# One shared priority, and a shorter planned lag, for the small operations of an inverse square root

## The chip, the cores and the metric

The kernel runs on one core of a Trainium2 chip. The metric is the device time of one execution in microseconds (us); the figure for the kernel before is the median of three runs. One more execution was profiled, and all rows below come from it.

## The reference

Two models of two layers each run on 256 tokens of width 1024, one behind the other. What matters here is that both normalise often, each time with 1/sqrt of a sum of squares:

```python
def rms_norm(x, g):
    xf = x.astype(jnp.float32)
    y = xf * lax.rsqrt(jnp.mean(xf * xf, -1, keepdims=True) + NORM_EPS)
    return (y * g.astype(jnp.float32)).astype(x.dtype)
...
    kk = kk / jnp.maximum(jnp.sqrt(jnp.sum(kk * kk, -1, keepdims=True)), 1e-12)    # rwkv7, per head
    y = (y - mean) * lax.rsqrt(var + RWKV_GN_EPS) * hv(ln_g) + hv(ln_b)            # rwkv7, per head
    o = ((o - mean) * lax.rsqrt(var + RET_GN_EPS)).reshape(b, s, h * dv) * gn_g.astype(f32)   # retention
...
    for l in range(DEPTH):                                   # first model
        h = rms_norm(x, attn_norm_g[l])
        ... attention over chosen keys, rwkv7, pooling, retention, gates, merge ...
        h2 = rms_norm(x, mlp_norm_g[l])
        x = x + jnp.square(jax.nn.relu(h2 @ mlp_up[l])) @ mlp_down[l]
```

The second model has the same kind of norms (of rows, of heads, of latents) around a gated delta rule with block attention, a latent attention, and two layers that mix many small experts ("peer").

## The kernel before

The activations stay on the chip; weights stream in as tiles of 128x1024 (tile `raw`). ScalarE rounds each tile into a high part (`hi`), VectorE takes the rest (`lo = raw - hi`), and TensorE multiplies three times (`hT`,`hi`; `lT`,`hi`; `hT`,`lo`) into PSUM tiles `mm` and `sm`. The instruction rows of TensorE are 128x256 matmuls nearly throughout.

In the span of the profiled execution the stages lie so: 20 to 440 us the mix of layer 0 of the first model, 470 to 660 its MLP, 660 to 1080 the mix of layer 1, 1080 to 1310 its MLP, 1310 to 1515 the gated delta rule and block attention of the second model, 1515 to 2360 the first peer layer, 2360 to 2495 the latent attention, 2495 to 3343 the second peer layer.

**An inverse square root is a chain of small VectorE operations.** `rsqrt` (line 467) is 10 operations that each need the one before: a bit trick, then three Newton steps; the last one writes the result spread out to 128x256 (`wide`). `head_rsqrt` puts one more ahead (`v`, which reads the sums from PSUM). `rstd` (line 586) does it for whole rows in 15 operations, of which two independent ones always stand together. There are 35 such chains: 20 of `head_rsqrt` (tile `h`, ten in each mix of the first model), 3 of `unit` in the delta rule (tiles `g8v`, `g8r`, `g8t`), 10 of `rstd` (tile `rs`), 2 of `unit` in the latent attention. Below they are numbered 0 to 34 in the order of VectorE's program.

**What sets the order.** The program is written as generators (rwkv7, attention, retention, the gates and so on), and a `Plan` gives every operation a planned start and end while it is issued: a cost by its size, and `LAG` (0.3 us) from the end of an operation of VectorE or ScalarE until its result counts as ready. Two orders come out of that:

- On VectorE and ScalarE a scheduler orders the instructions by the priority that `Noted.call` sets, the planned start (`cur_priority = 1000 + int(start * 1000)`); one that is not ready by the scheduler's reckoning lets a later one pass. So operations of other generators come to stand between two operations of a chain. They are called fillers below.
- TensorE's order is the order of issue. `weave` (line 775) takes up a generator when the planned time of TensorE reaches the time that the generator has yielded. `head_rsqrt` yields the end of its chain by the plan plus `HM` and then issues the transposes of the wide result, which need the whole chain:

```python
        s.rsqrt(rs, v, tm, wide)
        wide = wide.rearrange("p (t n e) f -> p t n (e f)", t=2, n=n)
        yield s.plan.last + s.HM
        ps = s.sm((P, n, S))
        for j in range(n):
            for t in range(2):
                nc.tensor.transpose(ps[:, j, t * P:(t + 1) * P], wide[:, t, j, :], s.ident)
```

The matmuls that TensorE has between those that make the sums and the first transposes are called the cover of a chain below. In the profile nearly all rows carry line 378, the call in `Noted.call`, and those issued under `issue_after` line 383; tiles tell them apart. A transpose reads as `sm<-cst,h`.

Of the kernel before, what the change touches and what calls it, by code (L numbers as in the profile page):

```python
# [2 lines left out]

# [1 line left out]

# [22 lines left out]
I32 = mybir.dt.int32  # L28
# [5 lines left out]
OP = mybir.AluOpType  # L34
# [5 lines left out]
D = 1024  # L40
# [89 lines left out]

PACE, ARENA = 2.0, 11776
SUMS, REST = 6, 8
NLAG = 1
ELATE, EN = 2, 4
TUNE = ((0.3, 0.2, 1.0), (0.3, 0.2, 1.0), (0.28, 0.25, 1.0), (0.3, 0.2, 1.0), (0.3, 0.2, 1.0), (0.3, 0.2, 1.0))
# [115 lines left out]
class Plan:  # L251
# [5 lines left out]
    def __init__(s, tc):  # L257
        s.tc = tc
        s.start = 0.0
        s.pe = 0.0  # L260
        s.dve = 0.0
        s.last = 0.0
        s.floor = 0.0
        s.after = {}
        s.busy = {}
        s.seen = {}
        s.slots = {}
        s.born = {}
        s.used = {}
# [30 lines left out]
    def cost(s, eng, op, out, ins):  # L300
# [17 lines left out]
            return 0.07 + n * 0.00052  # L318
        return 0.08 + n * (0.0063 if op == "reciprocal" else 0.00104)

    def put(s, eng, t, c):
        if eng == "PE":
            t = max(t, s.pe)
            s.pe = t + c
            return t + c
        q = s.busy.setdefault(eng, [])
        i = len(q)
        while i > 0 and q[i - 1][1] > t:
            i -= 1
        while i < len(q) and q[i][0] - t < c:  # L330
            t = max(t, q[i][1])
            i += 1
        q.insert(i, (t, t + c))
        if len(q) > 400:
            del q[:200]
        return t + c

    def note(s, eng, op, args, kw):
        aps = [x for x in list(args) + list(kw.values()) if hasattr(x, "tensor") and hasattr(x, "partition_size")]
        s.start = s.pe  # L340
        if not aps:
            return
        on = [x for x in aps if x.tensor.name in s.born]
        out = aps[0]
        name = out.tensor.name
        t = max(s.ready(*on), s.floor)
        t = max(t, s.born.get(name, 0.0))
        c = s.cost(eng, op, out, aps[1:])
        f = s.put(eng, t, c)
        s.start = f - c  # L350
        if eng == "DMA":
            f += 2.0
        for x in on:
            m = x.tensor.name
            s.used[m] = max(s.used.get(m, 0.0), f)
        for x in (out, kw.get("accum_out")):
            if x is not None and x.tensor.name in s.born:
                s.seen.setdefault(x.tensor.name, {})[s.box(x)] = f + (0.0 if eng == "PE" else s.LAG)
        s.last = max(s.last, f + s.LAG)
        if eng == "DVE":  # L360
            s.dve += c


class Noted:
# [5 lines left out]
    def __getattr__(s, name):  # L370
        f = getattr(s._e, name)

        def call(*args, **kw):
            s._p.note(s._k, name, args, kw)
            s._p.tc.cur_priority = 1000 + int(s._p.start * 1000)
            a = s._p.after.get(s._k)
            if a is None:
                return f(*args, **kw)  # L378
            a[1] -= 1
            if a[1] == 0:  # L380
                del s._p.after[s._k]
            with s._p.tc.issue_after(a[0]):
                return f(*args, **kw)  # L383

        s.__dict__[name] = call
        return call
# [14 lines left out]
class K:  # L401
# [65 lines left out]
    def rsqrt(s, out, v, tmp, wide=None):  # L467


        nc = s.nc  # L470
        nc.vector.tensor_scalar(out.bitcast(I32), v.bitcast(I32), -0.5, 1597463007.0, op0=OP.mult, op1=OP.add)
        for i in range(3):
            nc.vector.scalar_tensor_tensor(tmp, out, -0.5, out, op0=OP.mult, op1=OP.mult)
            nc.vector.tensor_tensor(tmp, tmp, v, op=OP.mult)
            if i == 2 and wide is not None:
                m = wide.shape[-1]
                w = lambda x: x.to_broadcast(list(x.shape[:-1]) + [m])
                nc.vector.scalar_tensor_tensor(wide, w(tmp), 1.5, w(out), op0=OP.add, op1=OP.mult)
            else:
                nc.vector.scalar_tensor_tensor(out, tmp, 1.5, out, op0=OP.add, op1=OP.mult)  # L480

    def setup(s):
        nc, I = s.nc, s.I
# [102 lines left out]
    def rstd(s, eps, eps2=None):  # L586


        nc = s.nc
        v, h, y, z = (s.t(s.pst, [P, 2], F, f"rs{i}", bufs=2) for i in range(4))  # L590
        nc.vector.tensor_scalar(v, s.ss[:, 0, :], 1.0 / D, eps, op0=OP.mult, op1=OP.add)
        if eps2 is not None:
            nc.vector.tensor_scalar(v, v, eps2, None, op0=OP.mult)
            nc.vector.scalar_tensor_tensor(v, s.ss[:, 1, :], 1.0 / D, v, op0=OP.mult, op1=OP.add)
        nc.vector.tensor_scalar(y.bitcast(I32), v.bitcast(I32), -0.5, 1597463007.0, op0=OP.mult, op1=OP.add)
        nc.vector.tensor_scalar(h, v, -0.5, None, op0=OP.mult)
        for i in range(3):
            for t in range(2):
                c = slice(t, t + 1)
                nc.vector.scalar_tensor_tensor(z[:, c], y[:, c], h[:, c], y[:, c], op0=OP.mult, op1=OP.mult)  # L600
            for t in range(2):
                c = slice(t, t + 1)
                nc.vector.scalar_tensor_tensor(y[:, c], z[:, c], 1.5, y[:, c], op0=OP.add, op1=OP.mult)
        return y

    def over(s, rs):
# [68 lines left out]
    def norm(s, rb, scale, bias=None, h=None):  # L675
# [4 lines left out]
        for k in range(8):  # L680
            u = s.tmp()
            if k > NLAG:
                s.plan.after["DVE"] = [i[k - NLAG - 1].ins, 1]
            c = scale[:, k:k + 1]
# [1843 lines left out]
```

## Time and profile before

| | |
|---|---|
| median of 3 runs | 3362.69 us (3359.47 to 3372.65) |
| the profiled execution | 3344.62 us |
| its span (first to last instruction) | 3342.8 us |
| mean granted clock of TensorE | 0.973 of full speed |
| TensorE busy | 3185.0 us, 95% |
| VectorE busy | 2446.3 us, 73% |
| ScalarE busy | 1733.2 us, 52% |

A busy time is the sum of an engine's instructions over the span. "Idle before" in a row is the time the engine stood still ahead of this instruction, with the instruction that released it behind the arrow.

### The profile page before, as it was taken

To read this page: it belongs to the slowest core of one execution; us is meant where nothing else is said; L and a number is where in the kernel's file an instruction comes from. 1 tells how busy PE (TensorE), PEld (TensorE's weight loads), DVE (VectorE), ACT (ScalarE), POOL (GpSimd) and SP (SyncE) were. 2 spreads that over 40 slices of the span, in tenths; PEclk is the share of its full clock that TensorE was granted. 3 is DMA by queue.
4 is the path that set the end of the run, shared out by engine and by line. 5 is a ranking of instruction groups with operands and counts; after the bars stand their busy time and mean duration, and the time that the engine had idled before them with its cause. 6 is when DMAs were issued, how large, how long until landed. Compare 5 with 4: busy or idle time off the path is not lost. (4 is left out here: it accounts for less than half of the span.)

```text
span 3342.8 us, 66312 instructions
## 1 busy us (share of the span) xinstructions
PE 3185.0 (95%) x27140; PEld 3090.1 (92%) x27140; DVE 2446.3 (73%) x4732; ACT 1733.2 (52%) x2836; POOL 157.1 (5%) x74
## 2 busy tenths in 40 slices
PE   7999999999899999899999999999899999999998
PEld 6988899989789999889999999999889999999998
DVE  7676677767757667966999767787566998677654
ACT  4444344444434445445457757644454558667543
POOL 0000000000000000000331000000001330000000
PEclk8999999999899999899999999999899999999999
DMA  5433377634233774325554556598335555555664
GB/s 174 132 96 95 95 244 256 198 119 121 82 101 118 249 256 154 120 68 180 173 170 157 170 163 196 188 352 290 123 108 178 176 158 165 175 160 166 190 188 139
DMA packets 151505, 555.00 MB, mean 166 GB/s; under 512 B 17697, under 2 KB 17697, under 8 KB 150177
## 3 DMA queue, kind: packets, MB, share of 16 engines
q1 hardware_dynamic: 151200, 550.77, 51.3%
q8 instruction: 212, 3.47, 0.4%
q14 instruction: 93, 0.75, 0.1%
HBM read 545.46 MB, written 5.24 MB: 165 GB/s over the span
## 5 line engine op out<-in xcount | busy, mean ns | idle before, releaser
L378 ACT CAST hi<-raw 128x1024 fp32r<-128x1024 f32 x906 | 950.9, 1050 | 1159.0 <-PE mm L378 559.0
L378 DVE TENSOR_TENSOR lo<-raw,hi 128x1024 fp32r<-128x1024 f32 x884 | 1118.5, 1267 | 571.8 <-ACT hi L378 562.0
L378 PE MATMUL mm<-hT,hi 128*128 128x256 f32 (+1 forms) x3688 | 1069.6, 290 | 0.1
L378 PE MATMUL mm<-hT,lo 128*128 128x256 f32 (+1 forms) x3688 | 1051.4, 285 | 15.3 <-DVE lo L378 15.2
L378 PE MATMUL mm<-lT,hi 128*128 128x256 f32 (+1 forms) x3688 | 1050.0, 285 | 15.4 <-DVE lT L378 14.7
L378 PEld LDWEIGHTS mm<-lT,hi 128*128 128x128 f32 x3688 | 707.7, 192 | 21.5 <-DVE lT L378 21.1
L378 PEld LDWEIGHTS mm<-hT,lo 128*128 128x128 f32 x3688 | 707.2, 192 | 17.9 <-DVE lo L378 17.6
L378 PEld LDWEIGHTS mm<-hT,hi 128*128 128x128 f32 x3688 | 707.5, 192 | 9.7 <-issue 7.7
L378 PE MATMUL sm<-lT,hi 128*128 128x256 f32 x2096 | 592.9, 283 | 6.5 <-DVE lT L378 6.4
L378 PE MATMUL sm<-hT,hi 128*128 128x256 f32 x2096 | 592.6, 283 | 3.4 <-ACT hT L378 3.2
L378 PE MATMUL sm<-hT,lo 128*128 128x256 f32 x2096 | 591.9, 282 | 2.7 <-DVE lo L378 2.6
L378 PEld LDWEIGHTS sm<-lT,hi 128*128 128x128 f32 x2096 | 397.0, 189 | 8.2 <-DVE lT L378 7.7
L378 PEld LDWEIGHTS sm<-hT,hi 128*128 128x128 f32 x2096 | 397.4, 190 | 4.0 <-ACT hT L378 3.4
L378 PEld LDWEIGHTS sm<-hT,lo 128*128 128x128 f32 x2096 | 396.2, 189 | 4.1 <-DVE lo L378 4.1
L378 PE MATMUL sm<-o,hi 128*128 128x256 f32 x768 | 189.1, 280 | 0.0
L378 PE MATMUL sm<-o,lo 128*128 128x256 f32 x640 | 179.7, 281 | 0.0
L378 ACT ACTIVATE x<-iota,x 128x128 f16<-128x128 f16 x512 | 163.1, 390 | 13.3 <-PE sm L378 13.3
L378 POOL TENSOR_TENSOR lo<-raw,hi 128x1024 fp32r<-128x1024 f32 x36 | 94.2, 2617 | 1182.4 <-ACT hi L378 1181.2
L378 PE MATMUL sm<-sq,hi 128*128 128x256 f32 x512 | 143.9, 281 | 1.1 <-DVE sq L378 1.1
L378 PEld LDWEIGHTS sm<-o,hi 128*128 128x128 f32 x768 | 135.7, 188 | 0.0
L378 PE MATMUL mm<-hi,hT 128*128 128x256 f32 (+1 forms) x416 | 124.0, 298 | 1.2 <-ACT hT L383 1.2
L378 PEld LDWEIGHTS sm<-o,lo 128*128 128x128 f32 x640 | 120.7, 189 | 0.0
(480 smaller groups left out, 4623.9 us busy)
## 6 DMA issues: line engine op xcount, KB each, us to landing
raw<-pu SPq DMA_DIRECT2D x256, 512.0 KB, 3.6
raw<-pw SPq DMA_DIRECT2D x256, 512.0 KB, 3.6
raw<-wf SPq DMA_DIRECT2D x108, 512.0 KB, 3.7
raw<-up SPq DMA_DIRECT2D x64, 512.0 KB, 4.3
raw<-dn SPq DMA_DIRECT2D x64, 512.0 KB, 4.3
o<-modw SPq DMA_DIRECT2D x48, 512.0 KB, 4.6
act<-modw SPq DMA_DIRECT2D x48, 512.0 KB, 5.4
raw<-wb SPq DMA_DIRECT2D x32, 512.0 KB, 3.6
```

The costliest lines, as they stand in the source:

```text
L378: return f(*args, **kw)
```

## The change

`Plan.chain()` is a context around the body of `rsqrt` and of `rstd`. Inside it every operation gets the priority of the first one's planned start (`pin`) instead of its own. Inside it, too, a result counts as ready `PINLAG` = 0.1 us after its operation instead of 0.3; the last operation gets its 0.3 back. For the 10 operations of `rsqrt` the plan's end so comes 9 x 0.2 = 1.8 us earlier, and with it the time that `head_rsqrt` yields. The `v` operation of `head_rsqrt` lies outside.

```diff
@@ class Plan
+PINLAG = 0.1
+        s.pin = None
...
+    @contextmanager
+    def chain(s):
+
+        s.pin = 0.0
+        yield
+        s.pin = None
+        s.tail[0][s.tail[1]] += s.LAG - PINLAG
...
-                s.seen.setdefault(x.tensor.name, {})[s.box(x)] = f + (0.0 if eng == "PE" else s.LAG)
+                lag = 0.0 if eng == "PE" else s.LAG if s.pin is None else PINLAG
+                s.tail = s.seen.setdefault(x.tensor.name, {}), s.box(x)
+                s.tail[0][s.tail[1]] = f + lag
@@ Noted.call
-            s._p.tc.cur_priority = 1000 + int(s._p.start * 1000)
+            if s._p.pin == 0.0:
+                s._p.pin = s._p.start
+            s._p.tc.cur_priority = 1000 + int((s._p.pin or s._p.start) * 1000)
@@ rsqrt, and rstd likewise
-        nc.vector.tensor_scalar(out.bitcast(I32), v.bitcast(I32), -0.5, 1597463007.0, op0=OP.mult, op1=OP.add)
-        for i in range(3):
...
+        with s.plan.chain():
+            nc.vector.tensor_scalar(out.bitcast(I32), v.bitcast(I32), -0.5, 1597463007.0, op0=OP.mult, op1=OP.add)
+            for i in range(3):
...
```

The instructions are the same before and now: 27043 of TensorE and 3733 of VectorE in the program. (The trace has more rows, since it records some of them in two.) TensorE's order differs in the two mixes of the first model and at the delta rule; from the first peer layer on it is the same. Counted over the two orders of instructions, for the chains where something differs (VectorE fillers between the first and the last operation, TensorE matmuls and transposes of others in the cover):

| chain | place, us | fillers before | now | cover before | now |
|---|---|---|---|---|---|
| 1 | 43 | 9 | 9 | 6 | 36 |
| 2 | 114 | 4 | 3 | 48 | 36 |
| 3 | 138 | 7 | 7 | 54 | 36 |
| 4 | 203 | 1 | 0 | 43 | 34 |
| 5 | 235 | 18 | 13 | 18 | 32 |
| 6 | 309 | 1 | 1 | 42 | 12 |
| 7 | 337 | 8 | 11 | 46 | 20 |
| 8 | 386 | 2 | 2 | 56 | 38 |
| 9 | 400 | 0 | 0 | 42 | 36 |
| 10 | 411 | 4 | 2 | 42 | 42 |
| 11 (`rs`) | 470 | 1 | 2 | 24 | 24 |
| 13 | 684 | 0 | 0 | 54 | 36 |
| 16 | 850 | 2 | 2 | 37 | 31 |
| 17 | 875 | 18 | 17 | 10 | 6 |
| 18 | 952 | 15 | 15 | 42 | 36 |
| 19 | 986 | 11 | 8 | 30 | 32 |
| 20 | 1030 | 2 | 2 | 46 | 38 |
| 21 | 1044 | 0 | 0 | 42 | 36 |
| 22 | 1056 | 3 | 2 | 60 | 42 |
| 25 (`rs`) | 1327 | 32 | 33 | 164 | 164 |
| 26 (`g8v`) | 1380 | 15 | 14 | 42 | 30 |
| 27 (`g8v`) | 1468 | 0 | 0 | 20 | 12 |
| 29, 33 (`rs`) | 1512, 2491 | 1, 1 | 0, 0 | 24, 24 | 24, 24 |
| all 35 | | 176 | 164 | 1244 | 1085 |

On VectorE in chain 1 (first mix, about 43 us; `h` is the chain, the rows with `ra`, `hs`, `m1s` and `kr` belong to rwkv7 and the pooling), the order before is:

```order
L378 TENSOR_SCALAR h_98_487<-sm_484 128x4
L378 TENSOR_SCALAR ra_530<-ra_530,hs_533 128x128
L383 SCALAR_TENSOR_TENSOR ra_424<-ra_425,ra_424 128x240
L378 TENSOR_SCALAR h_99_488<-h_98_487 128x4
L378 TENSOR_TENSOR ra_539<-ra_530,ra_452 128x256
L383 TENSOR_SCALAR ra_425<-ra_424 128x240
L378 SCALAR_TENSOR_TENSOR h_100_489<-h_99_488 128x4
L378 TENSOR_TENSOR kr_548<-ra_388,ra_543 128x2x128
L383 TENSOR_SCALAR ra_424<-ra_424 128x240
L378 TENSOR_TENSOR h_100_489<-h_100_489,h_98_487 128x4
```

and now it is:

```order
L392 TENSOR_SCALAR h_101_499<-sm_496 128x4
L392 TENSOR_TENSOR m1s_588<-hs_584 128x1
L397 SCALAR_TENSOR_TENSOR ra_424<-ra_425,ra_424 128x240
L392 TENSOR_TENSOR ra_590<-ra_581,ra_452 128x256
L392 TENSOR_SCALAR h_102_500<-h_101_499 128x4
L397 TENSOR_SCALAR ra_425<-ra_424 128x240
L392 TENSOR_TENSOR kr_599<-ra_388,ra_594 128x2x128
L392 SCALAR_TENSOR_TENSOR h_103_501<-h_102_500 128x4
L397 TENSOR_SCALAR ra_424<-ra_424 128x240
L392 TENSOR_TENSOR h_103_501<-h_103_501,h_101_499 128x4
L397 TENSOR_SCALAR ra_425<-ra_424 128x240
L392 SCALAR_TENSOR_TENSOR h_102_500<-h_103_501,h_102_500 128x4
```

Other operations still stand between those of the chain: about one after each.

On VectorE in chain 11 (the row norm ahead of the first MLP; `lo` is a weight's low part, `o` with `cond` a wide operation of 128x1024 on the second model's modulation), the order before is:

```order
L378 TENSOR_SCALAR rs_939_5101<-sm_5094 128x2
L378 TENSOR_SCALAR rs_941_5103<-rs_939_5101 128x2
L378 TENSOR_SCALAR rs_940_5102<-rs_939_5101 128x2
L378 TENSOR_TENSOR lo_5202<-raw_5200,hi_5201 128x1024
L378 SCALAR_TENSOR_TENSOR rs_942_5104<-rs_941_5103,rs_940_5102 128x1 x2
L378 SCALAR_TENSOR_TENSOR rs_941_5103<-rs_942_5104,rs_941_5103 128x1 x2
```

and now it is:

```order
L392 TENSOR_SCALAR rs_939_5101<-sm_5094 128x2
L392 TENSOR_SCALAR rs_941_5103<-rs_939_5101 128x2
L392 TENSOR_SCALAR rs_940_5102<-rs_939_5101 128x2
L392 TENSOR_TENSOR lo_5202<-raw_5200,hi_5201 128x1024
L397 SCALAR_TENSOR_TENSOR o_961_5224,mod_88_448<-o_961_5224,cond_5133 128x1024
L392 SCALAR_TENSOR_TENSOR rs_942_5104<-rs_941_5103,rs_940_5102 128x1 x2
L392 SCALAR_TENSOR_TENSOR rs_941_5103<-rs_942_5104,rs_941_5103 128x1 x2
```

The wide operation has moved into the chain, behind the `lo` that stood there already.

On TensorE in chain 17 (second mix, about 875 us; the `ra` matmuls make the sums, `sm` from `o` are four matmuls of the attention, `mm` a weight's, the last row the transposes of `h`), the order before is:

```order
L378 MATMUL sm_9713<-cst_77,ra_9710 128x2 x2
L378 MATMUL sm_9734<-o_1556_8954,o_1555_8953 128x256 x2
L378 MATMUL sm_9739<-o_1556_8954,o_1555_8953 128x256 x2
L378 MATMUL mm_9664<-hT_7421,hi_9745 128x256
L378 MATMUL mm_9664<-lT_7422,hi_9745 128x256
L378 MATMUL mm_9664<-hT_7421,lo_9746 128x256
L378 MATMUL mm_9664<-hT_7421,hi_9745 128x256
L378 MATMUL mm_9664<-lT_7422,hi_9745 128x256
L378 MATMUL mm_9664<-hT_7421,lo_9746 128x256
L378 MATMUL sm_9756<-cst_77,h_1697_9720 128x128 x2
```

and now it is:

```order
L392 MATMUL sm_9701<-cst_77,ra_9698 128x2 x2
L392 MATMUL mm_9656<-hT_7421,hi_9720 128x256
L392 MATMUL mm_9656<-lT_7422,hi_9720 128x256
L392 MATMUL mm_9656<-hT_7421,lo_9721 128x256
L392 MATMUL mm_9656<-hT_7421,hi_9720 128x256
L392 MATMUL mm_9656<-lT_7422,hi_9720 128x256
L392 MATMUL mm_9656<-hT_7421,lo_9721 128x256
L392 MATMUL sm_9731<-cst_77,h_1697_9708 128x128 x2
```

The four matmuls of the attention no longer stand between the sums and the transposes; the six of the weight do.

## Rows read from the trace of the kernel before

**Rows 1.** The page, busy time of each engine over the span.

```profile
PE 3185.0 (95%) x27140; PEld 3090.1 (92%) x27140; DVE 2446.3 (73%) x4732; ACT 1733.2 (52%) x2836; POOL 157.1 (5%) x74
```

**Rows 2.** The waits: engine, line, tile waited for; us in total, times, longest us.

```profile
PE sm L378 <- DVE h L378: 23.1, 8, 6.5
...
PE sm L378 <- DVE rs L378: 14.5, 7, 7.5
```

**Rows 3.** Timeline, PE: start, length, operation, [idle before, releaser], at eight first transposes.

```profile
48.72 0.45 PE L378 MATMUL sm<-cst,h 128*128 128x128 f32 x1 [4.74 <-DVE h L378]
...
242.66 0.45 PE L378 MATMUL sm<-cst,h 128*128 128x128 f32 x1 [6.52 <-DVE h L378]
...
417.38 0.30 PE L378 MATMUL sm<-cst,h 128*128 128x128 f32 x1 [1.23 <-DVE h L378]
...
474.29 0.32 PE L378 MATMUL sm<-cst,rs 128*128 128x128 f32 x1 [1.65 <-DVE rs L378]
...
882.60 0.47 PE L378 MATMUL sm<-cst,h 128*128 128x128 f32 x1 [5.00 <-DVE h L378]
...
961.04 0.45 PE L378 MATMUL sm<-cst,h 128*128 128x128 f32 x1 [4.15 <-DVE h L378]
...
1344.24 0.48 PE L378 MATMUL sm<-cst,rs 128*128 128x128 f32 x1 [7.50 <-DVE rs L378]
...
1388.20 0.32 PE L378 MATMUL sm<-cst,g8r 128*128 128x128 f32 x1 [1.73 <-DVE g8r L378]
```

**Rows 4.** Timeline, DVE: an undisturbed chain, first and last operation.

```profile
684.35 0.16 DVE L378 TENSOR_SCALAR h<-sm 128x4 f32<-128x4 f32 x1
...
686.33 0.43 DVE L378 SCALAR_TENSOR_TENSOR h<-h,h 128x256 f32<-128x256 f32 x1
```

**Rows 5.** Timeline, PE: the last two matmuls before the transposes of chain 1.

```profile
43.34 0.41 PE L378 MATMUL mm<-lT,hi 128*128 128x256 f32 x1
43.56 0.41 PE L378 MATMUL mm<-hT,lo 128*128 128x256 f32 x1
```

**Rows 6.** Timeline, PE: first matmul in the cover of chain 6, its first transpose.

```profile
308.44 0.36 PE L378 MATMUL mm<-hi,hT 128*128 128x256 f32 x1
...
313.48 0.27 PE L378 MATMUL sm<-cst,h 128*128 128x128 f32 x1
```

**Rows 7.** Timeline, DVE: chain 6, first operation, the filler in it, last operation.

```profile
309.13 0.15 DVE L378 TENSOR_SCALAR h<-sm 128x4 f32<-128x4 f32 x1
...
311.49 1.23 DVE L378 TENSOR_TENSOR lo<-raw,hi 128x1024 fp32r<-128x1024 f32 x1 [0.63 <-ACT hi L378]
...
312.83 0.42 DVE L378 SCALAR_TENSOR_TENSOR h<-h,h 128x256 f32<-128x256 f32 x1
```

**Rows 8.** Timeline, PE: f32 matmuls in the cover of chain 17.

```profile
873.64 2.39 PE L378 MATMUL sm<-o,o 64*128 64x256 f32 x8
```

**Rows 9.** Timeline, PE: small f32 matmuls in the cover of chain 19.

```profile
986.14 3.78 PE L378 MATMUL sm<-o 32*128 32x128 f32 x32
```

**Rows 10.** Timeline, DVE: chain 17, first two rows and the last.

```profile
875.18 0.14 DVE L378 TENSOR_SCALAR h<-sm 128x4 f32<-128x4 f32 x1
875.24 0.16 DVE L378 TENSOR_SCALAR hs<-ra 128x2 f32<-128x2 f32 x1
...
882.13 0.42 DVE L378 SCALAR_TENSOR_TENSOR h<-h,h 128x256 f32<-128x256 f32 x1
```

**Rows 11.** Timeline, DVE: chain 11, twelve paired operations, and a wide one after it.

```profile
472.92 1.44 DVE L378 SCALAR_TENSOR_TENSOR rs<-rs,rs 128x1 f32<-128x1 f32 x12
...
479.96 1.22 DVE L383 SCALAR_TENSOR_TENSOR o<-o,cond 128x1024 f32<-128x1024 f32 x1
```

**Rows 12.** Windows: length; busy PE, PEld, DVE, ACT, POOL, granted clock, DMA share, GB/s.

```profile
41.00:53.00 12.00, 6.79 (x32) 6.53 (x33) 9.07 (x38) 3.97 (x9) 0.00 (x0) 0.52 0.15 44
53.00:60.00 7.00, 7.00 (x60) 6.68 (x58) 3.47 (x4) 3.37 (x6) 0.00 (x0) 1.00 0.39 106
236.00:248.00 12.00, 5.48 (x31) 5.37 (x30) 11.93 (x46) 2.74 (x7) 0.00 (x0) 0.72 0.15 44
```

More of the change, by code (lines that the diff above doesn't have):

```diff
@@ L1 @@
 import math
-from contextlib import ExitStack
+from contextlib import ExitStack, contextmanager
 import numpy as np
@@ L470, in rsqrt @@
         nc = s.nc
-        nc.vector.tensor_scalar(out.bitcast(I32), v.bitcast(I32), -0.5, 1597463007.0, op0=OP.mult, op1=OP.add)
-        for i in range(3):
[L473 to L480, printed above, removed]
+        with s.plan.chain():
+            nc.vector.tensor_scalar(out.bitcast(I32), v.bitcast(I32), -0.5, 1597463007.0, op0=OP.mult, op1=OP.add)
+            for i in range(3):
+                nc.vector.scalar_tensor_tensor(tmp, out, -0.5, out, op0=OP.mult, op1=OP.mult)
+                nc.vector.tensor_tensor(tmp, tmp, v, op=OP.mult)
+                if i == 2 and wide is not None:
+                    m = wide.shape[-1]
+                    w = lambda x: x.to_broadcast(list(x.shape[:-1]) + [m])
+                    nc.vector.scalar_tensor_tensor(wide, w(tmp), 1.5, w(out), op0=OP.add, op1=OP.mult)
+                else:
+                    nc.vector.scalar_tensor_tensor(out, tmp, 1.5, out, op0=OP.add, op1=OP.mult)
     def setup(s):
@@ L590, in rstd @@
         v, h, y, z = (s.t(s.pst, [P, 2], F, f"rs{i}", bufs=2) for i in range(4))
[L591 to L603, printed above, removed]
+        with s.plan.chain():
+            nc.vector.tensor_scalar(v, s.ss[:, 0, :], 1.0 / D, eps, op0=OP.mult, op1=OP.add)
+            if eps2 is not None:
+                nc.vector.tensor_scalar(v, v, eps2, None, op0=OP.mult)
+                nc.vector.scalar_tensor_tensor(v, s.ss[:, 1, :], 1.0 / D, v, op0=OP.mult, op1=OP.add)
+            nc.vector.tensor_scalar(y.bitcast(I32), v.bitcast(I32), -0.5, 1597463007.0, op0=OP.mult, op1=OP.add)
+            nc.vector.tensor_scalar(h, v, -0.5, None, op0=OP.mult)
+            for i in range(3):
+                for t in range(2):
+                    c = slice(t, t + 1)
+                    nc.vector.scalar_tensor_tensor(z[:, c], y[:, c], h[:, c], y[:, c], op0=OP.mult, op1=OP.mult)
+                for t in range(2):
+                    c = slice(t, t + 1)
+                    nc.vector.scalar_tensor_tensor(y[:, c], z[:, c], 1.5, y[:, c], op0=OP.add, op1=OP.mult)
         return y
```

## The prediction

> **What bounds the kernel now.** I read the page first: TensorE is busy 95% of the span and VectorE 73% [rows 1], so a chain on VectorE costs time only where TensorE stands still for it. Then the chain of waits: TensorE waits for tile `h`, the result of `head_rsqrt`, eight times, 23.1 us in all, and for `rs` seven times, 14.5 us [rows 2]. The reader is to see how small that is: together 37.6 us, 1.1% of 3344.62. Then the timeline of TensorE at the transposes: five waits make up 21.6 of the 23.1 us, those of chains 1, 5, 10, 17 and 18 (4.74, 6.52, 1.23, 5.00, 4.15); those of chains 11, 25 and 26 are 1.65, 7.50 and 1.73 [rows 3]. Twelve of the twenty `h` chains end in time: their cover is longer than they are. Last the timeline of VectorE: undisturbed, a chain runs from 684.35 to 686.33, ten steps of 0.20, and ends after 2.4 us with its wide operation [rows 4]. So two lengths race at each chain, VectorE's (chain and fillers) and TensorE's (cover), and a wait is the first less the second.
>
> **What the change does to both.** By the order of instructions it closes the chains up hardly at all: 176 fillers before, 164 now, 115 and 104 of them in the `h` chains. A later operation of a chain has the first one's priority, but when a filler is ready and it is not, the filler still passes. The planner, however, believes in an end 1.8 us earlier, and so the transposes come earlier in TensorE's order: the cover falls from 1244 matmuls to 1085 (from 790 to 651 at `h`). Where there was reserve that costs nothing; where there was none a wait arises. Each term is the change of the wait at one chain, in us.
>
> Chain 1: the last two matmuls of its cover start 0.22 apart, at the lower clock level [rows 5]. Its cover grows from 6 to 36. The last ended about when the chain had 5.2 us to go (43.56 to 48.72 [rows 3, 5]); 30 more at 0.22 are 6.6, at full clock, 0.12, they are 3.6. The fillers stay at nine. I take the wait as gone: **-4.7**; with the fast matmuls a rest of 0.8 stays, -3.9.
>
> Chain 6: 42 matmuls lie between 308.44 and 313.48, 0.12 each [rows 6]; the chain runs from 309.13 to 312.83 + 0.42 = 313.25, with one `lo` in it [rows 7]. With a cover of 12 TensorE would be there at 308.44 + 12 x 0.12 = 309.88, so it waits 313.25 - 309.88 = **+3.4**. If the `lo`, 1.23, should not fall into it on the chip, +2.2.
>
> Chain 17: the four f32 matmuls that leave its cover took 2.39 [rows 8], and there are 17 fillers for 18, so **+1.5** between 0 (they were waiting beside it anyway) and 2.4; nearer the upper end, as its wait of 5.00 shows no reserve. Chain 18: six matmuls fewer, 6 x 0.12 = **+0.7** (0 at least).
>
> Chains 7 and 19 change roles. The cover of 7 falls from 46 to 20 and now holds 8 small matmuls and 12 of 32x128 such as 19 had before, where 16 of them (32 records) took 3.78 [rows 9]. Twelve make 2.8, the eight some 0.6, together 3.4, against 46 x 0.12 = 5.5 before: 2.1 less, and small operations take the place of `lo` on VectorE: **+2.0** (1.0 to 3.0). At 19 the filler of `lo` kind comes in as three small ones go: **+0.8** (0 to 1.6). Chain 26: twelve matmuls fewer, 1.4 at full clock and 2.6 at the lower, one filler fewer: **+1.6** (0 to 2.6).
>
> Chain 5: five fillers fewer, cover 18 to 32, but four transposes of the softmax now stand in the cover and wait for VectorE themselves; the wait mostly passes to them: **-0.5** (-2 to 0). Chain 10: two fillers fewer at the same cover, the wait of 1.23 goes: **-1.2** (up to 0).
>
> What is a filler worth? In chain 17 the next independent operation starts 0.06 after the chain's, at 875.24 after 875.18 [rows 10], where a dependent one starts after 0.20 [rows 4]: small fillers lie partly in the gaps, so taking one out frees less than its length. The Trainium skill ("VectorE: DVE Perf Modes", section "The DRAIN you can't avoid") says that an operation which is held starts only when the pipe is empty, and one that is not held starts earlier. By the page's rule alone the closed chain gains nothing on its own steps; the trace agrees, with the 0.20 and the 0.06.
>
> `rstd` already goes in pairs, twelve operations in 1.44, 0.12 apart [rows 11], and its covers stay (344). Chain 11 has a new filler, the operation of 128x1024 that stood at 479.96 and takes 1.22 [rows 11]; its chain ended 1.65 too late already [rows 3]: **+1.2** (0 if something else held it up). Chain 25 has one more, **+0.4** (0 at least), by the length of a 256-wide operation [rows 7]. At 29 and 33 a `lo` stands ahead of the chain now instead of in it: 0.
>
> The covers of 2, 3, 16 and 22 lose 12 + 18 + 6 + 18 = 54 matmuls, 6.5 us at 0.12. The three `h` waits that rows 3 do not show total 23.1 - 21.6 = 1.5, so most had a reserve, of unknown size: 0 to 6.5, and I take a third, **+2.3**, since two of the four lose a filler too. Chains 4, 8, 9, 13, 20 and 21 lose 6 to 18 matmuls each of 42 to 56, and each chain is nearly bare, at most two fillers: 36 remaining are 4.3 us against 2.4 + some 1.2: nothing. If that cover fails, each costs up to 1.
>
> **Sum**: -4.7 + 3.4 + 1.5 + 0.7 + 2.0 + 0.8 + 1.6 - 0.5 - 1.2 + 1.2 + 0.4 + 2.3 = +7.5. All lower ends give -4.7, all upper ends +17.9. Against the profiled execution that is 3344.62 + 7.5 = 3352.1. This execution lies 18 us (0.54%) under the median of the runs, so against that, 3362.7 + 7.5 = **3370**, with a range of its own of 3358 to 3381. About 0.5% (16.8 us) is what a measurement of this kernel can tell from no change: the forecast is no change that can be told.
>
> **The rivals.**
>
> *Slower, through the clock.* In 41 to 53, where TensorE stood still for chain 1 (busy 6.79 of 12), the granted clock was 0.52, near the 1.2 GHz level; in 53 to 60, busy throughout, 1.00; in 236 to 248, with chain 5's wait, 0.72 [rows 12]. If each of the new or longer waits (6, 7, 17, 18, 19, 26) drags the clock down likewise, it costs another 12 x (1 - 0.72) = 3.4 us, six times 20: +28, 3391. It decides from three such waits on with a fall behind them (+10, over half the way to 16.8). For it: 0.52 and 0.72. Against it: chains 17, 18 and 26 wait already, so their fall is paid for, and chain 1 may give one back. The Trainium skill ("TensorE: Matmul & The Clock Gate", section "HAM oscillation — how this bites in real kernels") tells of gaps that put the clock back each time round, so that every piece of work after them starts slow. [...] Chance 0.23.
>
> *Faster, the chains do close up.* If the chip runs them bare all the waits for `h` and `g8r` go, 23.1 + 1.7 = 24.8: 3338. Against it: 164 fillers stand in the order, and VectorE takes its instructions in that order. Chance 0.05.
>
> *Faster, chain 1 with its clock.* If its wait goes and TensorE runs at full clock there, that gives 4.7 and up to 12 x 0.48 = 5.8; if also the new waits are covered (their terms at the lower ends) and transposes that come earlier spare another 6 us of waits behind them, about -17: 3346. Against it: three things have to meet. Chance 0.08.
>
> **How the numbers follow.** The forecast has 0.64, the three rivals 0.23, 0.05 and 0.08. The predicted time is the forecast's, 3370. From 3346 to 3392 the range leaves out the first faster rival, half of the second and something under half of the slower one, with the tail of the forecast about 0.2. Faster by over 0.5% is 0.05 + 0.08 = 0.13, within 0.64, slower 0.23.
>
> **What would show it.** In the profile after: no wait at chain 1's transposes; a wait of 2 to 4 us at chain 6's and of 1 to 3 at chain 7's, where there was none; that of chain 17 over 5; that of chain 11 near 2.9, with the operation of 128x1024 between `rs` rows on VectorE. Waits for `h` should total 23.1 - 4.7 - 0.5 - 1.2 + 10.7 = 27 to 28 instead of 23.1. I am wrong if chains run with fillers out of the way (the waits for `h` under 10), if the granted clock falls behind the new waits, or if the time moves in the peer layers, where TensorE's order is the same.

## The result: 0.6% slower

The changed kernel takes 3383.31 us (median of 4 runs, 3376.25 to 3388.49), the kernel before in the same session 3362.31. The ratio is 1.0061, with a 95% interval of 1.0039 to 1.0084. The profiled execution, the slowest of the four, took 3388.49 us, with a span of 3386.7.

The page of the changed kernel, busy time of each engine:

```profile
PE 3220.6 (95%) x27140; PEld 3116.7 (92%) x27140; DVE 2450.9 (72%) x4732; ACT 1732.3 (51%) x2836; POOL 157.3 (5%) x74
```

The span less TensorE's busy time, that is, its time without work, is 3386.7 - 3220.6 = 166.1 us; before it was 3342.8 - 3185.0 = 157.8 [rows 1]. So TensorE stands still 8.3 us longer, about the 7.5 of the forecast. But it is also busy 35.6 us longer with the same instructions, and that was not in the sum. The chain of waits of the changed kernel (us in all, times, longest):

```profile
PE sm L392 <- DVE h L392: 23.2, 9, 7.4
...
PE sm L392 <- DVE sq L392: 14.2, 18, 2.0
PE sm L392 <- DVE rs L392: 14.1, 6, 7.9
PE sm L392 <- DVE o L392: 11.5, 6, 3.8
...
PE sm L392 <- DVE g8r L392: 3.3, 1, 3.3
```

In the kernel before, the waits for `sq` and `o` were shorter:

```profile
PE sm L378 <- DVE sq L378: 11.3, 16, 2.0
...
PE sm L378 <- DVE o L378: 6.4, 3, 2.7
```

The waits for `h` have the same sum as before [rows 2], in nine places instead of eight. TensorE's timeline at the transposes shows where they went (start, length, operation, idle before):

```profile
47.60 0.28 PE L392 MATMUL mm<-hT,lo 128*128 128x256 f32 x1
47.77 0.30 PE L392 MATMUL sm<-cst,h 128*128 128x128 f32 x1
...
321.27 0.30 PE L392 MATMUL sm<-cst,h 128*128 128x128 f32 x1 [3.69 <-DVE h L392]
...
349.85 0.44 PE L392 MATMUL sm<-cst,h 128*128 128x128 f32 x1 [2.48 <-DVE h L392]
...
904.40 0.48 PE L392 MATMUL sm<-cst,h 128*128 128x128 f32 x1 [7.40 <-DVE h L392]
...
983.87 0.45 PE L392 MATMUL sm<-cst,h 128*128 128x128 f32 x1 [5.70 <-DVE h L392]
...
1011.87 0.33 PE L392 MATMUL sm<-cst,h 128*128 128x128 f32 x1 [1.14 <-DVE h L392]
...
1377.69 0.47 PE L392 MATMUL sm<-cst,rs 128*128 128x128 f32 x1 [7.92 <-DVE rs L392]
...
1419.45 0.32 PE L392 MATMUL sm<-cst,g8r 128*128 128x128 f32 x1 [3.32 <-DVE g8r L392]
```

Chain 1 (47.77) waits no more. Chains 6 (321.27), 7 (349.85) and 19 (1011.87), which ended in time before, do now; 17, 18, 25 and 26 wait longer than in [rows 3]. And this is what happens behind the wait of chain 7. Windows of the changed kernel (length; busy PE, PEld, DVE, ACT, POOL; granted clock, DMA share, GB/s):

```profile
340.00:349.00 9.00, 6.94 (x74) 5.96 (x72) 8.68 (x33) 4.64 (x12) 0.30 (x1) 1.00 0.37 117
349.00:360.00 11.00, 10.15 (x38) 6.78 (x38) 4.14 (x13) 0.59 (x1) 0.00 (x0) 0.52 0.01 1
360.00:370.00 10.00, 10.00 (x39) 7.39 (x39) 1.26 (x2) 1.67 (x3) 0.00 (x0) 0.50 0.00 1
370.00:380.00 10.00, 10.00 (x85) 9.43 (x84) 7.14 (x11) 3.74 (x7) 0.00 (x0) 1.00 0.35 104
```

The same piece of the program in the kernel before:

```profile
342.00:352.00 10.00, 10.00 (x77) 7.36 (x77) 7.05 (x18) 1.07 (x3) 0.00 (x0) 1.00 0.29 100
```

What stands there are the small f32 matmuls of the retention. The granted clock goes to 0.50, that is 1.2 GHz, at the wait and stays there for 20 us, though from the end of the wait on TensorE is busy without a break (360 to 370: 10.00 of 10, 0.50). Where they ran at full clock they were through in about half the time (77 rows in 10 us, against 38 and 39 in 21). Slower work like this is the part that the prediction's sum does not have.

### The profile page after: what moved, and what is told of

Read it like the earlier page. It is cut to its first block, busy times and chain, and to the rows that moved or that the text cites. A ratio compares the mean times of both kernels' runs of the same rounds, so it can differ in the third digit from the quotient of the medians.

```text
span 3386.7 us, 66314 instructions
## 1 busy us (share of the span) xinstructions
PE 3220.6 (95%) x27140; PEld 3116.7 (92%) x27140; DVE 2450.9 (72%) x4732; ACT 1732.3 (51%) x2836; POOL 157.3 (5%) x74
## 5 line engine op out<-in xcount | busy, mean ns | idle before, releaser
L392 PEld LDWEIGHTS mm<-hT,lo 128*128 128x128 f32 x3688 | 710.5, 193 | 18.9 <-DVE lo L392 18.5
L392 PE MATMUL mm<-hi,lT 128*128 128x256 f32 (+1 forms) x416 | 120.8, 291 | 0.0
```

## The experiments

Before each experiment stood two questions: is it the shared priority or the planned lag, and is it the waits or the clock behind them. Time without work below is always span less busy time of TensorE from that run's page (the expectations count only the gaps between instructions, which is 6.5 us less: 159.6 for the changed kernel); the clock is the mean granted clock over the timed executions.

| run | ratio (95%) | span | busy | without work | mean clock |
|---|---|---|---|---|---|
| shared priority alone | 1.0001 (0.9982 to 1.0020) | 3361.7 | 3205.6 | 156.1 | 0.969 |
| shorter lag alone | 1.0078 (1.0054 to 1.0102) | 3384.3 | 3217.6 | 166.7 | 0.966 |
| change, transposes 1.8 us later | 1.0033 (1.0018 to 1.0047) | 3361.1 | 3197.8 | 163.3 | 0.969 |
| before, fillers queued behind chains | 1.0232 (1.0207 to 1.0257) | 3437.9 | 3226.0 | 211.9 | 0.962 |
| shorter lag, first mix | 1.0041 (1.0026 to 1.0056) | 3361.9 | 3201.3 | 160.6 | 0.968 |
| shorter lag, second mix | 1.0035 (1.0019 to 1.0051) | 3363.0 | 3201.4 | 161.6 | 0.969 |
| shorter lag, second model | 1.0020 (1.0004 to 1.0036) | 3351.4 | 3195.8 | 155.6 | 0.968 |
| change, waits filled | 1.0010 (0.9993 to 1.0027) | 3370.7 | 3222.4 | 148.3 | 0.974 |
| before, waits filled | 0.9972 (0.9955 to 0.9989) | 3347.3 | 3210.7 | 136.6 | 0.974 |
| before, more filled | 0.9966 (0.9946 to 0.9985) | 3361.4 | 3229.0 | 132.4 | 0.976 |
| change, retention filled | 1.0077 (1.0054 to 1.0100) | 3374.8 | 3206.5 | 168.3 | 0.969 |
| first mix, chains 6 and 7 filled | 0.9999 (0.9987 to 1.0010) | 3363.2 | 3209.6 | 153.6 | 0.971 |

In the filled ones busy contains the useless matmuls. A profile is one execution and can lie at either end of a kernel's runs: that of "before, more filled" was the slowest of 12, that of "change, waits filled" the second slowest, those of "transposes 1.8 us later", "first mix" and "second model" the fastest. So the busy time and the span in the table can't be set against the ratio beside them.

**Shared priority alone.** The lag is 0.3 everywhere again:

```diff
-PINLAG = 0.1
...
-        s.tail[0][s.tail[1]] += s.LAG - PINLAG
...
-                lag = 0.0 if eng == "PE" else s.LAG if s.pin is None else PINLAG
+                lag = 0.0 if eng == "PE" else s.LAG
```

> The change without its shorter lag: the operations of a chain share one priority, the plan counts 0.3 us after each as before. Theory (the lag does it all): the order of instructions on TensorE and VectorE is that of the kernel before, row for row, so the time is the same, ratio 1.000 within 0.002, and waits for h stay near 23 us. Rival (the shared priority is what costs): ratio 1.004 to 1.008. It also gives a second profile of the old order: if the span of 3342.8 us at a granted clock of 0.973 was a lucky execution, this one has a clock of 0.966 to 0.970 and 3355 to 3370 us.

The order of instructions on TensorE and VectorE is that of the kernel before, row for row: giving the operations of a chain one priority moves nothing at all. The ratio is 1.0001. The run also answers the question of the profile: the same program has here a span of 3361.7, 18.9 more than the profiled execution of before, 20.6 of that in TensorE's busy time. In its windows the retention of the first mix is slow here too, though no wait like chain 7's new one stands ahead of it (TensorE is busy 9.83 of the 10 us before):

```profile
335.00:345.00 10.00, 9.83 (x103) 9.28 (x102) 8.94 (x31) 5.20 (x13) 0.00 (x0) 0.99 0.48 145
345.00:355.00 10.00, 10.00 (x36) 6.30 (x36) 4.09 (x12) 0.59 (x1) 0.00 (x0) 0.50 0.11 42
355.00:365.00 10.00, 10.00 (x41) 6.89 (x41) 0.67 (x2) 1.70 (x4) 0.00 (x0) 0.50 0.00 0
```

So in the old order this stretch falls to the lower level in some executions and in others not, and it can fall without a wait.

**Shorter lag alone.** Each operation has its own start as priority again:

```diff
-            s._p.tc.cur_priority = 1000 + int((s._p.pin or s._p.start) * 1000)
+            s._p.tc.cur_priority = 1000 + int(s._p.start * 1000)
```

> The change without the shared priority: each operation keeps its own planned start as priority, the plan counts 0.1 us inside a chain. Theory: the order of instructions is that of the changed kernel, row for row, so ratio 1.006 within 0.002, idle time of TensorE about 160 us, waits for h about 23 us in nine waits. Rival (the shared priority is what costs): ratio 1.000.

The order of instructions is that of the changed kernel, row for row, and so is the time. All that follows is the planner's lag. Against the run above, the same two orders in one session: without work 166.7 - 156.1 = +10.6, busy 3217.6 - 3205.6 = +12.0, span +22.6. Half of the loss is waiting, half is slower work. In this pair the first mix adds to neither half: it stands still as long as before (38.6 and 38.9 us of 0 to 450), and its retention is slow in both profiles. The second mix stands still 35.2 us instead of 27.2 (660 to 1110), and its retention is slow for 20 us (1016 to 1036) instead of 7 (1000 to 1007).

**Transposes 1.8 us later.**

```diff
-        yield s.plan.last + s.HM
+        yield s.plan.last + s.HM + 1.8
```

> The changed kernel, but head_rsqrt yields 1.8 us later, so that the transposes of the h chains go back to about where they stood on TensorE (cover of all chains 1240 matmuls, before 1244, changed 1085). Theory (the cut cover costs): the waits at chains 6, 7 and 19 go, chain 1 keeps none, idle time of TensorE falls from 159.6 to 148 to 154 us, ratio to before 0.997 to 1.002. Rival (the different order of the rest, or the clock by chance, costs): ratio stays 1.004 to 1.008.

Half a miss. The total cover is back, and about half of the loss is gone (1.0033 against 1.0078 in the same session). The wait at chain 19 is gone, those at 6 and 7 are 1.1 and 1.3 us; but chains 4, 5 and 10 wait 3.9, 4.3 and 2.6 us now, presumably since the weave takes turns at other places (not shown). The time without work stays 7 us over that of the old order. One number for all chains did not put the cover back.

**Fillers queued behind the chains.** This is what the change's words say, done in the kernel before:

```diff
...
-                nc.vector.scalar_tensor_tensor(wide, w(tmp), 1.5, w(out), op0=OP.add, op1=OP.mult)
+                i = nc.vector.scalar_tensor_tensor(wide, w(tmp), 1.5, w(out), op0=OP.add, op1=OP.mult)
             else:
-                nc.vector.scalar_tensor_tensor(out, tmp, 1.5, out, op0=OP.add, op1=OP.mult)
+                i = nc.vector.scalar_tensor_tensor(out, tmp, 1.5, out, op0=OP.add, op1=OP.mult)
+        s.plan.after["DVE"] = [i.ins, 20]
```

> The kernel before, with the next 20 VectorE operations issued after a chain of rsqrt queued behind the chain's last operation: 60 fillers instead of 176, the order of TensorE as before. This does what the change's words say. Theory (fillers are what the waits for h are made of): chains 5, 17 and 18 lose about 14, 15 and 15 fillers, their waits of 6.5, 5.0 and 4.2 us fall to under 2, waits for h in all from 23 to under 10, g8r from 1.7 to under 1; against that weights' lo operations come later by up to 2.4 us a chain and TensorE waits for some of them, 0 to 10 us. Ratio 0.994 to 0.999. Rival (the fillers are needed just as soon as the chain): the waits move to lo, ra and o, idle time stays 150 us or more, ratio 0.999 to 1.004.

It is 2.3% slower. The waits for `h` are gone from the chain of waits, and two that were not there stand in it, one at its head:

```profile
PE mm L378 <- DVE lo L383: 58.6, 21, 4.8
...
PE sm L378 <- DVE o L383: 13.0, 3, 9.1
```

Line 383 holds the operations that are issued behind another; two of the `lo` stood there before and 89 do now. At chain 5 TensorE now stops within the cover, at 243.08, for a weight's `lo` that VectorE began only at 241.80, after the chain:

```profile
243.08 0.58 PE L378 MATMUL mm<-hT,lo 128*128 128x256 f32 x1 [3.95 <-DVE lo L383]
```

Both theories were short of it. The fillers do lengthen the chains, for the waits for `h` go without them; but they also make what the matmuls of the cover read, and that comes too late now. This is one length of queue, twenty operations; a shorter one was not run.

**The lag in one part only** (`s.plan.pinlag` in place of `PINLAG`, set where the plan's part begins; 0 and 1 are the two mixes, above 1 the second model):

```diff
         s.plan.LAG, s.MARGIN, s.HM = TUNE[n]
+        s.plan.pinlag = PINLAG if n == 0 else s.plan.LAG
```

> The shorter lag only while the plan of the first mix is made (chains 1 to 10), 0.3 us everywhere else. Theory (the new waits cost, and each stands by itself): chains 1, 5 and 10 gain 4.7 + 2.8 + 1.1 = 8.6 us of waits, chains 6 and 7 lose 3.7 + 2.3, small ones 0.5, so idle time in all 147 to 150 us, as before; ratio 0.998 to 1.001. Rival (the granted clock falls behind the new waits): idle time the same, but 7 to 15 us more at the lower clock between 320 and 420 us; ratio 1.002 to 1.005.

> The shorter lag only in the second mix (chains 13 to 22). Theory: the waits at chains 14, 17, 18 and 19 grow by 0.9 + 2.4 + 1.6 + 1.1 = 6 us and nothing gains, so idle time in 660 to 1100 goes from 27 to 34 or 35, in all 156 to 158; with the clock behind them ratio 1.003 to 1.006. Rival (the loss belongs to the first mix or to the delta rule): 0.999 to 1.002.

> The shorter lag only in the second model (chains 24 to 34). Theory (the loss lies in the two mixes, 0.41% and 0.35%): chain 26 waits 1.6 us longer, nothing else moves; ratio 0.999 to 1.002. Rival (part of the loss sits here): 1.003 or more.

The first two lose 0.41% and 0.35%, the third 0.20% with an interval that nearly reaches 1; the sum, 0.96%, agrees with 0.78% within the intervals. In the first mix the ratio is the rival's: what chains 1, 5 and 10 gain pays for chains 6 and 7 (time without work in 0 to 450: 39.6 us, and 38.9 in "shared priority alone"), and still it loses 0.41%, 12 us in the medians (3373.96 to 3361.91). Its whole time without work is over both forecasts, 4.5 us more than in "shared priority alone", 2.9 of it in the second mix, where the order is the old one. In the second mix alone the mean clock is, to three digits, that of the kernel before (0.969): the clock's part there can't be read off it.

**Waits filled.** Useless matmuls of 128x256 ahead of the transposes, whose place they write to:

```diff
         ps = s.sm((P, n, S))
+        s.nh = getattr(s, "nh", 0) + 1
+        for _ in range({6: 26, 7: 16, 12: 10, 15: 52, 16: 42, 17: 6}.get(s.nh, 0)):
+            nc.tensor._e.matmul(ps[:, 0, :], s.h[0][0][:, :P], s.h[0][0], start=True, stop=True)
```

(the matmuls bypass the plan: TensorE's order is otherwise the same, and VectorE's differs in 42 of 4732 rows in the changed kernel; the numbers count the `h` chains; for the kernel before `{1: 20, 5: 46, 10: 7, 15: 36, 16: 30}`)

> The changed kernel with useless matmuls of 128x256 ahead of the transposes at six chains (26 at 6, 16 at 7, 10 at 14, 52 at 17, 42 at 18, 6 at 19: about what TensorE stands still there, at 0.12 us each); the transposes overwrite their result. Theory (half of the loss is the clock that falls behind the new waits): TensorE's time at the lower clock falls, cost of it while busy from 95 to 99 us to 78 to 88; the ends of the chains do not move; ratio 1.001 to 1.004 instead of 1.006 to 1.008. Rival (the clock falls for other reasons): ratio 1.006 or more.

> The kernel before with useless matmuls likewise at its own waits (20 at chain 1, 46 at 5, 7 at 10, 36 at 17, 30 at 18). Theory (clock): low spells behind 240, 880 and 960 us go, 8 to 15 us less, ratio 0.995 to 0.998. Rival (the clock falls for other reasons, or the matmuls delay the transposes where TensorE is slow): 0.999 to 1.003.

The useless matmuls give no result sooner, but with them the 0.6 to 0.8% of the changed kernel are gone but for 0.1%; the mean clock goes from 0.966 to 0.974. Waiting with work in TensorE costs less here than waiting without. This is not to say that the whole loss was the clock: the kernel before becomes 0.28% faster by the same, since some of the waits filled are old ones, and so faster than either kernel. Filled against filled, in one session, the changed order still loses 13.1 us (3362.51 to 3349.4), and its profile has 11.7 us more without work (148.3 to 136.6). So waits and clock each have about half, as in the pair above.

The profile of the changed kernel so filled has one thing that the theory does not have. Its retention in the first mix is at full clock, but that in the second mix is not, though the waits at chains 17, 18 and 19 are filled:

```profile
351.00:361.00 10.00, 10.00 (x69) 7.08 (x68) 3.66 (x11) 1.67 (x3) 0.00 (x0) 1.00 0.00 0
1003.00:1013.00 10.00, 10.00 (x36) 6.15 (x36) 3.60 (x8) 1.63 (x2) 0.00 (x0) 0.50 0.18 52
```

This execution lies 10 us over the median of its 12 runs; whether the others kept the clock there is not shown.

A few more at the same waits, and forty-eight at chain 25:

> The kernel before with useless matmuls at chains 1, 5, 10, 17 and 18 as in the run before, a few more each (24, 52, 9, 40, 33), and 48 more ahead of the transposes of chain 25, where TensorE waits 7.5 us. Theory: the low spell of 10 us at chain 25 (1339 to 1350 in the profile of before) shrinks to 3 or none, another 2 to 5 us less: ratio 0.994 to 0.997. Rival (enough was filled already, more only delays): 0.997 to 1.000.

In the profile the clock is at 1.00 from 1340 to 1370, the wait of chain 25 included, but the ratio, 0.9966, can't be told from 0.9972; nothing follows on the time that chain 25 costs.

**Retention filled.** Four useless matmuls at a time inside the slow stretch of the changed kernel, none at the waits:

```diff
                     h = 2 * (i + 2 * j) + e
+                    if j == 0:
+                        for _ in range(4):
+                            nc.tensor._e.matmul(ps[:, 1, :], s.h[0][0][:, :P], s.h[0][0], start=True, stop=True)
```

> The changed kernel with 16 useless matmuls of 128x256 in each of the two stretches of small f32 matmuls of the retention (those that read tile st), four at a time, and none at the transposes; the stretch overwrites their results. All waits stay as in the changed kernel. In the changed order both stretches ran at 1.2 GHz (st matmuls 0.42 to 0.47 us, 349 to 370 and 1015 to 1036), in the old order mostly at 2.4 (0.27 to 0.32). Theory (these two stretches are most of the clock's part): both run at full clock, 7 to 8 us less each, 4 us spent on the useless matmuls; ratio 1.003 to 1.005. Rival (the stretches are slow only because of the waits ahead of them, and matmuls inside them do not bring the clock back): ratio 1.007 to 1.009.

My theory fell: the ratio, 1.0077, is the rival's. In the first mix the stretch stays at the lower level, useless matmuls and all (1.22 for four, and `st` pairs of 0.69):

```profile
350.87 0.66 PE L392 MATMUL sm<-cst,h 128*128 128x128 f32 x2 [2.49 <-DVE h L392]
...
353.46 1.22 PE L1375 MATMUL sm<-hT 128*128 128x256 f32 x4
...
355.66 0.69 PE L392 MATMUL sm<-qd,st 32*64 32x128 f32 x2
```

In the second mix the clock was at 0.83 and 1.00 in that execution, with the waits ahead as they were. So what is filled in later does not reliably bring the clock back.

**First mix, chains 6 and 7 filled.** The lag in the first mix alone, with `{6: 26, 7: 16}` as above.

> The kernel with the shorter lag in the first mix alone (1.0041), with 26 useless matmuls ahead of the transposes of chain 6 and 16 ahead of those of chain 7, the two new waits of that mix. Idle time there was no more than before, so theory (the loss of the first mix is the clock that falls at the wait of chain 7 and stays down through the small f32 matmuls behind it) gives: that stretch at full clock, st matmuls of the first mix 0.27 to 0.32 us, ratio 0.999 to 1.002. Rival (the order of the first mix costs in other ways): ratio 1.003 to 1.006 still.

With 42 useless matmuls the 0.41% become -0.01%. The same stretch, behind a wait that is filled:

```profile
345.76 3.48 PE L1436 MATMUL sm<-hT 128*128 128x256 f32 x16
349.05 0.63 PE L393 MATMUL sm<-cst,h 128*128 128x128 f32 x2
...
351.27 0.43 PE L393 MATMUL sm<-qd,st 32*64 32x128 f32 x2
352.21 0.43 PE L393 MATMUL sm<-qd,st 32*64 32x128 f32 x2
```

The pairs take 0.43 instead of 0.68 and come every 0.94 us instead of 1.66.

**The two stretches in all the profiles.** The `st` matmuls of the retention tell the level: on the mean of the 16 in a mix they take 0.29 to 0.31 us or 0.44. Where each run stands (the two runs that are left out have another order on TensorE or VectorE, and take 0.29 us in both mixes):

| | 0.29 to 0.31 us | 0.44 us |
|---|---|---|
| first mix, old order | before; before, waits filled; lag in second mix; lag in second model | shared priority alone; before, more filled |
| first mix, new order | none | the changed kernel; shorter lag alone; lag in first mix; change, retention filled |
| first mix, new order, waits filled | change, waits filled; lag in first mix, chains 6 and 7 filled | none |
| second mix, old order | before; before, waits filled; shared priority alone; lag in first mix; lag in first mix, chains 6 and 7 filled; lag in second model | before, more filled |
| second mix, new order | change, retention filled | the changed kernel; shorter lag alone; lag in second mix |
| second mix, new order, waits filled | none | change, waits filled |

Each entry is one execution. In the first mix the stretch is slow in all four profiles of the new order with the wait at chain 7 unfilled, in neither of the two with it filled, and in two of six of the old order, which has no such wait. In the second mix filling the waits did not keep the clock in the one profile that there is.

## Why the prediction was right in its sum and wrong in its verdict

**That the change closes no chain up** was right, and more so than I wrote: by itself the shared priority moves no instruction (ratio 1.0001). The twelve fillers fewer come from the lag.

**The terms of the sum**, forecast and measured (wait after less wait before): chain 1 -4.7, -4.7; chain 6 +3.4, +3.7; chain 7 +2.0, +2.3; chain 17 +1.5, +2.4; chain 18 +0.7, +1.6; chain 19 +0.8, +1.1; chain 25 +0.4, +0.4; chain 26 +1.6, +1.6. Chain 5 was undersized: its 6.5 go, and 3.8 come back at the softmax's transposes (the `o` in the chain of waits), -2.7 instead of -0.5. Chain 10 -1.2, -1.2; chains 2, 3, 16 and 22 together +2.3, +0.4. Chain 11 can't be read off one pair of profiles: here it is -0.5 instead of +1.2. The operation of 128x1024 did come into the chain, on VectorE at 488.24, and the chain took longer by it, but its cover fell into a stretch at the lower clock (486 to 489) and took longer still. In the second pair, with both covers at the lower clock, it is +1.2: no wait in "shared priority alone", 1.16 in "shorter lag alone".

```profile
485.81 0.15 DVE L392 TENSOR_SCALAR rs<-sm 128x2 f32<-128x2 f32 x1
...
488.24 1.22 DVE L397 SCALAR_TENSOR_TENSOR o<-o,cond 128x1024 f32<-128x1024 f32 x1
```

In all, +7.5 forecast and +8.3 (+10.6 in the second pair) measured. That the sums lie so close is in part luck: the terms of the forecast measure +4.4 together, and the rest lies in waits that it put at nothing, above all those for `sq` (11.3 to 14.2 us) and chain 14 (0.70 to 1.57). The method of cover against chain holds at the single chains with large terms, 1, 6, 7 and 10, less well at 5, 17, 18 and the four small covers.

**What failed is the step that held the clock apart as a rival at 0.23.** The likeliest case, no change that can be told, is not what happened: 1.0061 lies 0.1% over the bound, with an interval that still takes the bound in, and the order of the changed kernel run again gives 1.0078, whose interval (from 1.0054) does not. The rival named the mechanism, that the new or longer waits drag the clock down, with 20 us for six waits and 28 in all; 21 came (25 in the second pair of medians, 3387.88 to 3362.61), where the profiles have about half as waiting and half, 12.0, as slower work. So the rival had the kind of cost right and its size, 20 us, too high; the forecast, which had nothing for it, was too low. Its price per wait, 3.4, was read off a wait that has 128x256 matmuls behind it. At chain 7 small f32 matmuls stand behind it, and the fall lasts 20 us. At chain 6 weight matmuls stand behind the wait, and the clock is back within 5 us:

```profile
321.60:326.00 4.40, 4.40 (x25) 4.35 (x24) 2.10 (x5) 0.95 (x3) 0.00 (x0) 0.61 0.10 42
326.00:340.00 14.00, 14.00 (x120) 14.00 (x120) 6.77 (x8) 6.54 (x10) 0.00 (x0) 1.00 0.51 151
```

So what was missing in the working is a look at what TensorE does after a new wait, not only at the wait. The wait is not the whole cause either: the stretch behind chain 7 was slow without it in two of six profiles of the old order.

The Trainium skill ("TensorE: Matmul & The Clock Gate", section "HAM oscillation — how this bites in real kernels") lays slow work to gaps in which TensorE has nothing to do. The trace agrees at chain 7, where the clock falls at a gap of 2.48 us, and in the first mix the loss is gone with the gaps at chains 6 and 7 filled (0.9999). It does not agree in "shared priority alone", where the same stretch falls to 0.50 at 345 with TensorE busy before and after; there the measurement decides.

**The forecast for the rival "the chains do close up"**, 3338 us, was wrong by its sign: where most of the fillers were put behind the chains, it took 3439.88. That step took the waits for `h` as all there is to gain and forgot who else waits for the fillers.

**The base** was off by luck: the profiled execution of before, 18 us under the median, was one in which the retention of the first mix ran at full clock. By the windows of "shared priority alone" (20 us at 0.50) that is worth about 10 us, an estimate; where the rest lies is open. I carried the sum over to the median, which was right, but a single profile could not show that this stretch is on the edge.

What stays open: why the same order falls to the lower level in some executions at chain 7 (the profiles of "shared priority alone" and "before, more filled") and not in others; why the second mix's retention stays slow behind filled waits; and how much of the second mix's 0.35% is its wait and how much the clock, which no run filled apart.

## What to carry to other kernels

A planner's lag is not a neutral number: make a chain look shorter and its consumer moves up in the order of the engine that it feeds, and the cover that hid it is gone. Before a wait is moved, look at what the engine does behind it: behind a wait of 2.5 us, a stretch of small matmuls took 20 us instead of 10. Compare a filled kernel with a filled one, or the gain on old waits hides the cost of the new ones. And in this scheduler a priority only chooses among operations that are ready (the shared one moved nothing); to hold others back took a queue edge, and then they were late where they were needed.

## What the runs showed of the hardware

The granted clock stayed at 0.50 for 20 us while TensorE was busy all the time, with f32 matmuls of 32 to 128 rows (350 to 370 and 1015 to 1036 in the changed kernel), and it fell there with no gap ahead in "shared priority alone" (9.83 of 10 us busy, then 0.50 from 345 to 365). Executions of one and the same program differ mostly by the clock: the twelve of "shared priority alone" run from 3345.77 us at a mean clock of 0.974 to 3368.54 at 0.966, and of the 18.9 us between the two profiles of the old order none is waiting. And useless matmuls in waits were worth having here: 139 of them, written over at once, made the kernel before 0.28% faster (0.9972, 0.9955 to 0.9989).
